# Differential attention of layer 1: when queries, keys and values are loaded, and how many gate steps run beside the first head

## The chip, the core and the metric

One core of a Trainium2 chip runs the whole program, a two-layer encoder trunk for 2048 tokens of width 1024, in float32. The metric is the device time of one execution in microseconds, as a median of several runs. The engines are named as in the profile: PE multiplies matrices, ACT evaluates functions and copies out of PSUM, DVE reduces and combines, POOL does elementwise work in SBUF, and SP issues the DMA transfers, in one queue and in order.

## The reference

Layer 0 is two kinds of chunked attention and is not touched by the change. Layer 1 is differential attention: each of 8 heads has two score maps, and the second is subtracted from the first with a learned weight.

```
def differential_attention(q1, q2, k1, k2, v, lam):
    ...
        s1 = jnp.einsum('bqhd,bkhd->bhqk', qb1, k1).astype(jnp.float32) * scale
        s2 = jnp.einsum('bqhd,bkhd->bhqk', qb2, k2).astype(jnp.float32) * scale
        p1 = jax.nn.softmax(jnp.where(mask, s1, NEG_INF), axis=-1)
        p2 = jax.nn.softmax(jnp.where(mask, s2, NEG_INF), axis=-1)
        a = p1 - lam * p2
        return jnp.einsum('bhqk,bkhd->bqhd', a.astype(v.dtype), v)
...
    o = rms_norm(o, subln_g) * (1.0 - lambda_init)
    y = (o.reshape(b, s, C_W) * jax.nn.silu(gate)) @ w_out
    return x + y
```

The mask lets a query see every key up to the end of its own chunk of 64 tokens.

## The kernel before

A float32 product is made of three products of rounded parts (`mm3`, lines 214 to 216: high by high, high by low, low by high). For scores it is two, because a query tile holds the same 64 rows twice and a key tile holds high and low parts in its two halves (lines 865 and 866).

Layer 1 has two stages. `_project` normalizes the tokens and makes queries, keys and values, which go to scratch in HBM. `_mix1` does all the rest; it begins where the projection's last matmul ends and is 38% of the program.

In `_mix1` the tokens are four blocks `b` of 512, taken from the last to the first, 3, 2, 1, 0. For each block come the 8 heads `h`. A head needs queries of its block (512 tokens) and all keys and values up to the end of the block, in pieces `z` of 512 tokens: four pieces in block 3, three in block 2. For each of four row tiles `j` of 128 queries and each of two maps `m`, `scores` makes a chunk of up to 128x512 per piece in PSUM (4 banks), DVE takes the row maximum (line 869), ACT the exponential (line 872), and POOL and DVE combine the two maps (lines 893 to 899). `values` then transposes the combined rows on PE (line 912), splits them (lines 915, 916) and multiplies them with the values (lines 919 to 921). `gate` multiplies the result with the gate of the head and normalizes it.

Beside the heads runs a side job, `gates()`: the gate part of the input projection, which `_project` leaves out. For each block it makes 8 columns of 128 outputs. A column is 8 steps of three matmuls (`cG`, lines 214 to 216), one PSUM bank, and a copy by ACT to SBUF (line 1033), which goes to HBM. In a block's last column each step is followed by the loads of two 128x512 tiles of the next block's normalized tokens over those just used (`p1hH<-hH`, `p1hL<-hL`, lines 1027 and 1028): 16 loads of 256 KB, called hidden loads below.

Three things set the order. First, `pace` draws from three generators: `heads()`, the queue of `values`, which trails the scores by `LAG1` units (20 in block 3), and the side job. Progress `u` is the mean of the units of scores and of values done; a head has 58 units in block 3 and 42 in block 2. The table `STAGES1` says how many side steps are to be done at each `u`, straight lines between its points:

```
    STAGES1 = ((0, 0), (600, 288), (780, 360), (1000, 440), (1088, 520))
...
        while sided < share((done + trailed) / 2) and next(side, None):
            sided += 1
```

Second, that order is a priority. A scheduler lays the instructions onto the engines by a model of their durations and moves one ahead when what it needs is free in that model; what it wrote is fixed in the program, and each engine runs its list in order. Third, buffers: a tile has a fixed number of places, and a load into a place waits on SP until the readers of the old content are done. Keys have 4 places for each map (`kp`, tags `k0`, `k1`), which in block 3 is exactly one head's keys; values have 4 pairs (`vp`), queries 2 (`ld`), gate weights 3 pairs of half columns. While SP waits for a place, all that stands behind it in the list waits too.

Before the change, `heads()` calls `load` for all pieces of a head (keys of map 0, keys of map 1, then values, piece by piece, lines 982 to 1000), and then `scores`, which begins with the eight loads of its queries (lines 841 to 847).

Of the kernel before, what the change touches and what calls it, by code (L numbers as in the profile page):

```python
# [11 lines left out]
F32R = mybir.dt.float32r  # L12
# [6 lines left out]
P = 128  # L19
# [3 lines left out]
NTB = 4  # L23
BLK = NTB * P
NB = S // BLK
HD = 64
# [5 lines left out]
def f32(ap):  # L32
    return ap.bitcast(F32)
# [52 lines left out]
class Trunk:  # L86
# [727 lines left out]
    def _mix1(self, es):  # L814
        nc, tc, a, s = self.nc, self.tc, self.a, self.s1
        n = "c"
# [7 lines left out]
        kp = pool("kp", 4)  # L824
# [10 lines left out]

        count = [0]

        def scores(h, b, K, res):

            tok = slice(b * BLK, (b + 1) * BLK)  # L840
            qd = ld.tile([P, 2, BLK], F32R, tag="qd", name=n + "qd")
            ql = ld.tile([P, 2, BLK], F32R, tag="ql", name=n + "ql")
            for m in range(2):
                r = slice(m * HD, (m + 1) * HD)
                for part, q in (("qH", qd), ("qL", ql)):
                    nc.sync.dma_start(f32(q[0:HD, m, :]), s[part][h, r, tok])
                    nc.sync.dma_start(f32(q[HD:P, m, :]), s[part][h, r, tok])
            us = res["u"] = []
            for j in range(NTB):
                t = b * NTB + j  # L850
                nk = (t + 1) * P
                cuts = [(c, min(nk, c + 512)) for c in range(0, nk, 512)]
                nb = len(cuts)
                js = slice(j * P, (j + 1) * P)
                nm, la, e = small("nm", 8), small("la", 8), small("e", 8)
                nm, la, e = (x.rearrange("p (m z) -> p m z", m=2) for x in (nm, la, e))
                l, rl = small("l", 2), small("rl", 2)
                rows = []
                for m in range(2):
                    chunks = []  # L860
                    for z, (c, ce) in enumerate(cuts):
                        wd = ce - c
                        ps = pS.tile([P, 512], F32, tag="S", name=n + "S")[:, :wd]
                        kt = K[z][m]
                        mm(ps, qd[:, m, js], kt[:, :wd], start=True, stop=False)  # L865
                        self.anchor = mm(ps, ql[:, m, js], kt[:, :wd], start=False, stop=True).ins  # L866
                        if ce == nk:
                            nc.vector.memset(ps[0:HD, wd - 64:], NEG)
                        nc.vector.tensor_reduce(nm[:, m, z:z + 1], ps, AX.X, ALU.max, negate=True)  # L869
                        chunks.append((sb if m else pp).tile([P, 512], F32, tag=f"P{m}", name=n + f"P{m}", bufs=6 if m else None))  # L870
                        acc = la[:, m, z:z + 1] if nb > 1 else l[:, m:m + 1]
                        nc.scalar.activation(chunks[z][:, :wd], ps, AF.Exp, bias=nm[:, m, z:z + 1], accum_out=acc)  # L872
                        yield wd / 256
                    rows.append(chunks)
                if nb > 1:
                    top, pe = small("top", 2), small("pe", 8).rearrange("p (m z) -> p m z", m=2)[:, :, :nb]
                    nc.vector.tensor_reduce(top, nm[:, :, :nb], AX.X, ALU.min)
                    for m in range(2):
# [23 lines left out]
        def values(h, b, V, res):  # L902
            us = res["u"]
            O = pO.tile([P, BLK], F32, tag="O", name=n + "O")
            nkt = (b + 1) * NTB
            for kt in range(nkt):
                j0 = max(0, kt - b * NTB)
                wd = (NTB - j0) * P
                tp = ptr.tile([P, 512], F32, tag="tr", name=n + "tr")
                kk = (kt % 4) * P  # L910
                for j in range(j0, NTB):
                    nc.tensor.transpose(tp[:, (j - j0) * P:(j - j0 + 1) * P], us[j][kt // 4][:, kk:kk + P], self.ident)  # L912
# [5 lines left out]
                vH, vL = (v[:, kk:kk + P] for v in V[kt // 4])  # L918
                mm(o, vH, H[:, :wd], start=(kt == 0), stop=False, skip_group_check=True)
                mm(o, vH, L[:, :wd], start=False, stop=False, skip_group_check=True)  # L920
                mm(o, vL, H[:, :wd], start=False, stop=(kt == nkt - 1), skip_group_check=True)
                if kt == 2:
                    while normal:
                        normal.pop(0)()
                yield wd / P
            gate(h, b, O)
# [52 lines left out]
                    split(h, b, o)  # L979
                    yield 1  # L980

        def load(h, i, K, V):

            tok = slice(i * BLK, (i + 1) * BLK)
            ks = []
            for m in range(2):
                k = kp.tile([P, BLK], F32R, tag=f"k{m}", name=n + f"k{m}")
                r, o = slice(m * HD, (m + 1) * HD), slice((1 - m) * HD, (2 - m) * HD)
                nc.sync.dma_start(f32(k[r, :]), s["kH"][h, r, tok])
                nc.sync.dma_start(f32(k[o, :]), s["kL"][h, r, tok])  # L990
                ks.append(k)
            K.append(ks)
            vs = []
            for part in ("vH", "vL"):
                v = vp.tile([P, BLK], F32R, tag=part, name=n + part)
                nc.sync.dma_start(
                    f32(v).rearrange("p (t c) -> p t c", t=NTB), s[part][tok, h * P:(h + 1) * P].rearrange("(t p) c -> p t c", p=P)
                )
                vs.append(v)
            V.append(vs)  # L1000

        room = self.last_hidden
        ended = set()
# [90 lines left out]
        queue = []  # L1094
        at = [NB - 1]

        def heads():
            for b in reversed(range(NB)):
                at[0] = b
                for h in range(8):  # L1100
                    K, V = [], []
                    for i in range(b + 1):
                        load(h, i, K, V)
                    res = {}
                    yield from scores(h, b, K, res)
                    queue.append(values(h, b, V, res))
            queue.append(leave())

        def leave():
# [58 lines left out]
```

## Time and profile before

| | |
|---|---|
| median of three runs | 2955.78 us (2952.22 to 2972.79) |
| the profiled execution | 2951.96 us, of which the span is 2950.2 us |
| PE, DVE, ACT, POOL busy, share of the span | 92%, 65%, 54%, 54% |
| mean granted clock of PE | 0.972 |
| last matmul of the projection begins | 1826.68 us |
| first score of head 0, 1, 2, 3, 4 of block 3 | 1840.48, 1875.51, 1926.21, 1979.29, 2041.03 us |
| first score of head 5, 6, 7 of block 3 | 2093.59, 2143.97, 2196.98 us |
| first score of block 2, of block 1 | 2248.42, 2550.78 us |

Times of single events are microseconds from the start of the span. A busy PE is not PE at its peak: the shown length of a 128x512 matmul is 0.39 us, but the next one begins 0.23 us after it.

### The profile page before, as it was taken

The numbers are of one execution on the slowest core, as the hardware profiler recorded it, in microseconds if no ns is written. First come the engines' busy times: TensorE is split into PE (matmuls) and PEld (weight loads), VectorE is DVE, ScalarE is ACT, GpSimd is POOL, SyncE is SP. The second block draws the span as 40 slices with busy tenths as digits, with TensorE's granted clock in tenths as the row PEclk, the third lists the DMA queues.
The fourth block names the chain that finished last, engine by engine and source line by source line (L and its number), as shares of the span: only waits on it lengthen the run. The fifth ranks groups of instructions, "written<-read, shape, count | busy, mean of one in ns | idle before, by whom it ended". The sixth has DMA issues, their size and how long they took to land.

```text
span 2950.2 us, 45159 instructions
## 1 busy us (share of the span) xinstructions
PE 2718.6 (92%) x13672; PEld 2242.1 (76%) x13672; DVE 1917.2 (65%) x4652; ACT 1593.5 (54%) x4135; POOL 1604.6 (54%) x1966
## 2 busy tenths in 40 slices
PE   6999999988888889899999998889999999899888
PEld 5888888876777788777788886667777777677667
DVE  7752385266677676498818861665766888878752
ACT  4443543367556565243334331666766777778752
POOL 3541251245345343267745650776777878789851
PEclk9999999999999999999999998999999999999999
DMA  4773343669988886475895455576768777668863
GB/s 149 230 250 120 113 147 120 197 192 249 262 214 212 216 217 170 146 270 197 259 302 191 127 162 158 164 217 197 225 193 234 200 225 214 176 169 243 221 215 114
DMA packets 427537, 580.79 MB, mean 197 GB/s; under 512 B 48160, under 2 KB 198688, under 8 KB 427296
## 3 DMA queue, kind: packets, MB, share of 16 engines
q1 hardware_dynamic: 427296, 577.92, 66.7%
q8 instruction: 109, 1.79, 0.3%
q14 instruction: 132, 1.08, 0.1%
HBM read 413.14 MB, written 164.63 MB: 196 GB/s over the span
## 4 chain that ended last, share of the span: by engine, by line
PE 63%; DMA 15%; DVE 11%; ACT 4%; POOL 3%; issue 3%; SPq 2%; DVEq 0%; ACTq 0%; POOLq 0%
PE p1mm L216 4%; PE p1mm L214 4%; PE p1mm L215 4%; PE p0mm L215 3%; PE p0mm L216 3%; PE p0mm L214 3%; PE cS L865 3%; PE ctr L912 3%; PE cS L866 3%; DMA mks<-bkL 2%; PE cO L920 2%; PE cG L214 2%; PE cG L216 2%; PE com L214 2%; DVE cnm L869 2%
## 5 line engine op out<-in xcount | busy, mean ns | idle before, releaser
L872 ACT ACTIVATE cP<-cS,cnm 128x512 f32<-128x512 f32 (+3 forms) x640 | 399.0, 630 | 173.8 <-DVE cnm L869 96.0
L869 DVE TENSOR_REDUCE cnm<-cS 128x1 f32<-128x512 f32 (+3 forms) x640 | 374.3, 600 | 100.6 <-PE cS L866 95.4
L865 PE MATMUL cS<-ck,cqd 128*128 128x512 f32 (+3 forms) x640 | 262.9, 415 | 60.0 <-ACT cP L872 20.5
L304 POOL TENSOR_TENSOR p0wL<-p0ws,p0wH 128x512 fp32r<-128x512 f32 (+1 forms) x128 | 155.3, 1246 | 276.0 <-ACT p0wH L303 266.4
L216 PE MATMUL p1mm<-p1wH,p1hL 128*128 128x512 f32 x768 | 303.3, 395 | 0.0
L215 PE MATMUL p1mm<-p1wL,p1hH 128*128 128x512 f32 x768 | 302.9, 395 | 0.4 <-POOL p1wL L304 0.4
L214 PE MATMUL p1mm<-p1wH,p1hH 128*128 128x512 f32 x768 | 302.3, 395 | 0.8 <-ACT p1wH L303 0.8
L899 POOL TENSOR_TENSOR cP<-cP,cP 128x512 f32<-128x512 f32 (+3 forms) x256 | 285.2, 1135 | 0.3
L304 POOL TENSOR_TENSOR p1wL<-p1ws,p1wH 128x512 fp32r<-128x512 f32 x128 | 168.0, 1333 | 136.8 <-ACT p1wH L303 97.5
L214 PE MATMUL p0mm<-p0wH,p0hH 128*128 128x512 f32 (+1 forms) x640 | 237.6, 374 | 3.5 <-ACT p0vt L454 2.6
L866 PE MATMUL cS<-ck,cql 128*128 128x512 f32 (+3 forms) x640 | 235.3, 372 | 3.3 <-DMA cql<-qL 3.3
L215 PE MATMUL p0mm<-p0wL,p0hH 128*128 128x512 f32 (+1 forms) x640 | 238.2, 373 | 0.0
L216 PE MATMUL p0mm<-p0wH,p0hL 128*128 128x512 f32 (+1 forms) x640 | 237.7, 372 | 0.1
L916 DVE TENSOR_TENSOR cptL<-ctr,cptH 128x512 fp32r<-128x512 f32 (+1 forms) x320 | 190.7, 599 | 62.4 <-ACT cptH L915 61.4
L865 PEld LDWEIGHTS cS<-ck,cqd 128*128 128x128 f32 x640 | 123.2, 193 | 104.4 <-ACT cP L872 51.2
L915 ACT ACTIVATE cptH<-ctr 128x512 fp32r<-128x512 f32 (+1 forms) x320 | 169.6, 539 | 58.2 <-PE ctr L912 57.0
L893 POOL TENSOR_SCALAR cP<-cP,ccs 128x512 f32<-128x512 f32 (+3 forms) x288 | 191.9, 683 | 0.0
L912 PE MATMUL ctr<-ident,cP 128*128 128x128 f32 x1088 | 175.4, 277 | 1.4 <-POOL cP L899 1.2
L898 POOL TENSOR_SCALAR cP<-cP,ccs 128x512 f32<-128x512 f32 (+3 forms) x256 | 174.0, 693 | 0.0
L214 PEld LDWEIGHTS p1mm<-p1wH,p1hH 128*128 128x128 f32 x768 | 145.3, 189 | 29.9 <-ACT p1wH L303 1.2
L215 PEld LDWEIGHTS p1mm<-p1wL,p1hH 128*128 128x128 f32 x768 | 145.2, 189 | 29.9 <-POOL p1wL L304 0.8
L216 PEld LDWEIGHTS p1mm<-p1wH,p1hL 128*128 128x128 f32 x768 | 145.4, 189 | 29.3 <-issue 0.2
(321 smaller groups left out, 7719.0 us busy)
## 6 DMA issues: line engine op xcount, KB each, us to landing
p1ws<-in_od_w_in_dram SPq DMA_DIRECT2D x56, 512.0 KB, 4.7
p0ws<-in_ev_w_in_dram SPq DMA_DIRECT2D x48, 512.0 KB, 4.3
ck<-kH SPq DMA_DIRECT2D x160, 128.0 KB, 4.0
ck<-kL SPq DMA_DIRECT2D x160, 128.0 KB, 4.2
cvH<-vH SPq DMA_DIRECT2D x80, 256.0 KB, 3.9
cvL<-vL SPq DMA_DIRECT2D x80, 256.0 KB, 4.7
cqd<-qH SPq DMA_DIRECT2D x128, 128.0 KB, 4.9
cql<-qL SPq DMA_DIRECT2D x128, 128.0 KB, 4.7
```

Of the source, the lines that this page charges most:

```text
L214: mm(ps, aH, bH, start=first, stop=False)
L215: mm(ps, aH, bL, start=False, stop=False)
L216: mm(ps, aL, bH, start=False, stop=last)
L304: nc.gpsimd.tensor_tensor(l[:, :width], ws[:, k, :width], f32(h[:, :width]), ALU.subtract)
L865: mm(ps, qd[:, m, js], kt[:, :wd], start=True, stop=False)
L866: self.anchor = mm(ps, ql[:, m, js], kt[:, :wd], start=False, stop=True).ins
L869: nc.vector.tensor_reduce(nm[:, m, z:z + 1], ps, AX.X, ALU.max, negate=True)
L872: nc.scalar.activation(chunks[z][:, :wd], ps, AF.Exp, bias=nm[:, m, z:z + 1], accum_out=acc)
L893: nc.gpsimd.tensor_scalar(p1, p1, c1, 1.0, ALU.mult, ALU.mult)
L899: nc.gpsimd.tensor_tensor(p1, p1, p2, ALU.add)
L912: nc.tensor.transpose(tp[:, (j - j0) * P:(j - j0 + 1) * P], us[j][kt // 4][:, kk:kk + P], self.ident)
L916: nc.vector.tensor_tensor(L[:, :wd], tp[:, :wd], f32(H[:, :wd]), ALU.subtract)
```

## The change

Three things are edited. The first head's queries are loaded ahead of its keys, and the loads of a head move into the scores of the head before it, through a function `then` that `scores` calls after each chunk: at the first chunk of row tile 2 the next head's queries; in row tile 3, after each chunk, the next head's keys of that map and piece, and at chunks of map 0 also the values of the present head. So the program's order of the keys is now all pieces of map 0, then all of map 1, which is the order of their use. Last, `STAGES1` gets a point: 45 side steps by `u` = 32, where the line before gave 15.

```
-    STAGES1 = ((0, 0), (600, 288), (780, 360), (1000, 440), (1088, 520))
+    STAGES1 = ((0, 0), (32, 45), (600, 288), (780, 360), (1000, 440), (1088, 520))
...
-        def scores(h, b, K, res):
-
+        def load_q(h, b):
             tok = slice(b * BLK, (b + 1) * BLK)
...
+            return qd, ql
+
+        def scores(h, b, q, K, res, then):
...
                         nc.scalar.activation(chunks[z][:, :wd], ps, AF.Exp, bias=nm[:, m, z:z + 1], accum_out=acc)
+                        then(j, m, z)
                         yield wd / 256
...
-        def load(h, i, K, V):
+        def load_k(h, i, m):
...
+        def load_v(h, i):
...
         def heads():
-            for b in reversed(range(NB)):
+
+
+            order = [(h, b) for b in reversed(range(NB)) for h in range(8)]
+            q, K = load_q(*order[0]), {(i, m): load_k(0, i, m) for m in range(2) for i in range(NB)}
+            for (h, b), nxt in zip(order, order[1:] + [None]):
                 at[0] = b
-                for h in range(8):
-                    K, V = [], []
-                    for i in range(b + 1):
-                        load(h, i, K, V)
-                    res = {}
-                    yield from scores(h, b, K, res)
-                    queue.append(values(h, b, V, res))
+                after, res = [None, {}], {"v": []}
+
+                def then(j, m, z):
+                    if (j, m, z) == (2, 0, 0) and nxt:
+                        after[0] = load_q(*nxt)
+                    if j == NTB - 1:
+                        if nxt and z <= nxt[1]:
+                            after[1][z, m] = load_k(nxt[0], z, m)
+                        if m == 0:
+                            res["v"].append(load_v(h, z))
+
+                yield from scores(h, b, q, K, res, then)
+                queue.append(values(h, b, res))
+                q, K = after
             queue.append(leave())
```

The first place is SP's list where the projection ends. `vH` and `vL` are the projection's own stores of values, `cvH` and `cvL` loads of values, `cqd` and `cql` loads of queries, `cwH` and `cwL` of gate weights. Before:

```order
L996 DMA cvH_21096<-vH_74 128x4x128
L996 DMA cvL_21098<-vL_75 128x4x128
L467 DMA vH_74<-p1vH_21038 128x512
L468 DMA vL_75<-p1vL_21039 128x512
L996 DMA cvH_21106<-vH_74 128x4x128
L996 DMA cvL_21108<-vL_75 128x4x128
L996 DMA cvH_21116<-vH_74 128x4x128
L996 DMA cvL_21118<-vL_75 128x4x128
L996 DMA cvH_21126<-vH_74 128x4x128
L996 DMA cvL_21128<-vL_75 128x4x128
L846 DMA cqd_21130<-qH_70 64x512
L847 DMA cqd_21130<-qH_70 64x512
```

Now, at the same place:

```order
L845 DMA cqd_21090<-qH_70 64x512
L846 DMA cqd_21090<-qH_70 64x512
L467 DMA vH_74<-p1vH_21038 128x512
L468 DMA vL_75<-p1vL_21039 128x512
L845 DMA cql_21091<-qL_71 64x512
L846 DMA cql_21091<-qL_71 64x512
```

The eight loads of values ahead of the first query are gone from here; they stand behind the queries of the second head. After the rows shown come the other four query loads and then the first gate weights.

The second place is PE's list in the first head, third row tile, map 0, second and third piece of keys (`ck0`). Before:

```order
L865 MATMUL cS_21336<-ck0_21100,cqd_21130 128x512
L866 MATMUL cS_21336<-ck0_21100,cql_21131 128x512
L214 MATMUL cG_21151<-p1hH_18326,cwH_21252 128x512
L215 MATMUL cG_21151<-p1hL_18327,cwH_21252 128x512
L216 MATMUL cG_21151<-p1hH_18326,cwL_21254 128x512
L865 MATMUL cS_21345<-ck0_21110,cqd_21130 128x512
L866 MATMUL cS_21345<-ck0_21110,cql_21131 128x512
L865 MATMUL cS_21351<-ck0_21120,cqd_21130 128x384
L866 MATMUL cS_21351<-ck0_21120,cql_21131 128x384
L865 MATMUL cS_21361<-ck1_21093,cqd_21130 128x512
L866 MATMUL cS_21361<-ck1_21093,cql_21131 128x512
```

Now:

```order
L870 MATMUL cS_21386<-ck0_21103,cqd_21090 128x512
L871 MATMUL cS_21386<-ck0_21103,cql_21091 128x512
L214 MATMUL cG_21322<-p1hH_18326,cwH_21323 128x512
L215 MATMUL cG_21322<-p1hL_18327,cwH_21323 128x512
L216 MATMUL cG_21322<-p1hH_18326,cwL_21325 128x512
L870 MATMUL cS_21395<-ck0_21106,cqd_21090 128x512
L871 MATMUL cS_21395<-ck0_21106,cql_21091 128x512
L214 MATMUL cG_21322<-p1hH_18326,cwH_21401 128x512
L215 MATMUL cG_21322<-p1hL_18327,cwH_21401 128x512
L216 MATMUL cG_21322<-p1hH_18326,cwL_21403 128x512
```

One step of gates stood between these chunks; now there is one after each chunk, and two behind the second. In the whole first head there are 110 gate matmuls where there were 39.

The third place is SP's list where the first hidden loads fall among the keys of a head. Before, that is the keys of head 3 (`ck0` map 0, `ck1` map 1). The row right ahead of these is the load of the first half of `ck0_22887`, its third piece of map 0:

```order
L1027 DMA p1hH_18326<-hH_78 128x512
L1028 DMA p1hL_18327<-hL_79 128x512 x2
L1027 DMA p1hH_18326<-hH_78 128x512
L989 DMA ck1_22870<-kH_72 64x512
L996 DMA cvH_22202<-vH_74 128x4x128
L996 DMA cvL_22204<-vL_75 128x4x128
L990 DMA ck1_22870<-kL_73 64x512
L1027 DMA p1hH_18326<-hH_78 128x512
L1028 DMA p1hL_18327<-hL_79 128x512
L989 DMA ck1_22880<-kH_72 64x512
L990 DMA ck1_22880<-kL_73 64x512
L990 DMA ck0_22887<-kL_73 64x512
```

Now the first hidden loads fall one head earlier, among the keys of head 2:

```order
L993 DMA ck0_22205<-kH_72 64x512
L994 DMA ck0_22205<-kL_73 64x512
L993 DMA ck0_22218<-kH_72 64x512
L994 DMA ck0_22218<-kL_73 64x512
L993 DMA ck0_22231<-kH_72 64x512
L994 DMA ck0_22231<-kL_73 64x512
L1033 DMA p1hH_18326<-hH_78 128x512
L1002 DMA cvH_22234<-vH_74 128x4x128
L1002 DMA cvL_22236<-vL_75 128x4x128
L1034 DMA p1hL_18327<-hL_79 128x512
L993 DMA ck0_22250<-kH_72 64x512
L994 DMA ck0_22250<-kL_73 64x512
```

Before, pieces of map 1 and hidden loads stand between the halves of a piece of map 0; now the pieces of map 0 stand together and ahead of map 1, and hidden loads and values stand among them. In the program before, one of three rounds of hidden loads stands among the keys of a head like this; now all three do, in whole or in part, among the keys of heads 2 and 5 of block 3 and of head 0 of block 2. From head 4 of block 2 on, PE's list holds the same work head by head, but for small shifts in block 1 and at the last two heads.

More of the change, by code (lines that the diff above doesn't have):

```diff
@@ L847, in scores @@
                     nc.sync.dma_start(f32(q[HD:P, m, :]), s[part][h, r, tok])
+            return qd, ql
+        def scores(h, b, q, K, res, then):
+            qd, ql = q
             us = res["u"] = []
@@ L863, in scores @@
                         ps = pS.tile([P, 512], F32, tag="S", name=n + "S")[:, :wd]
-                        kt = K[z][m]
+                        kt = K[z, m]
                         mm(ps, qd[:, m, js], kt[:, :wd], start=True, stop=False)
@@ L900, in scores, with values @@
                 us.append(rows[0])
-        def values(h, b, V, res):
+        def values(h, b, res):
             us = res["u"]
@@ L917, in values @@
                 o = O[:, j0 * P:]
-                vH, vL = (v[:, kk:kk + P] for v in V[kt // 4])
+                vH, vL = (v[:, kk:kk + P] for v in res["v"][kt // 4])
                 mm(o, vH, H[:, :wd], start=(kt == 0), stop=False, skip_group_check=True)
@@ L980, in fetch @@
                     yield 1
-        def load(h, i, K, V):
+        def load_k(h, i, m):
             tok = slice(i * BLK, (i + 1) * BLK)
[L985 to L992, printed above, removed]
+            k = kp.tile([P, BLK], F32R, tag=f"k{m}", name=n + f"k{m}")
+            r, o = slice(m * HD, (m + 1) * HD), slice((1 - m) * HD, (2 - m) * HD)
+            nc.sync.dma_start(f32(k[r, :]), s["kH"][h, r, tok])
+            nc.sync.dma_start(f32(k[o, :]), s["kL"][h, r, tok])
+            return k
+        def load_v(h, i):
+            tok = slice(i * BLK, (i + 1) * BLK)
             vs = []
@@ L999, in load @@
                 vs.append(v)
-            V.append(vs)
+            return vs
         room = self.last_hidden
```

## The prediction

> **What bounds the kernel now.** I read first the busy time by stretch, cut at the first score of each head of block 3, since the change acts there. Columns: the stretch, its length, then PE, PE weight loads, DVE, ACT and POOL busy with their instructions, granted clock, share of the DMA engines, GB/s.
>
> ```profile
> 1826.90:1840.48 13.58, 0.17 (x1) 0.03 (x1) 0.69 (x1) 0.60 (x1) 0.00 (x0) 0.58 0.97 251
> 1840.48:1875.51 35.03, 30.19 (x107) 20.34 (x107) 22.28 (x53) 22.48 (x68) 18.02 (x27) 0.87 0.53 162
> 1875.51:1926.21 50.70, 47.54 (x233) 37.90 (x233) 33.69 (x73) 33.54 (x92) 39.47 (x55) 1.00 0.60 172
> 1926.21:1979.29 53.08, 49.51 (x248) 39.50 (x247) 35.58 (x80) 36.18 (x97) 35.94 (x47) 1.00 0.76 214
> 1979.29:2041.03 61.74, 52.58 (x251) 41.70 (x248) 35.53 (x77) 36.65 (x99) 44.60 (x62) 0.92 0.71 201
> 2041.03:2093.59 52.56, 50.01 (x248) 39.20 (x246) 34.70 (x79) 35.84 (x99) 38.94 (x52) 1.00 0.63 179
> 2093.59:2143.97 50.38, 49.84 (x251) 39.75 (x250) 35.40 (x77) 35.53 (x98) 36.17 (x49) 1.00 0.87 270
> 2143.97:2196.98 53.01, 49.91 (x243) 40.11 (x241) 35.67 (x78) 35.50 (x98) 43.20 (x57) 0.97 0.65 181
> 2196.98:2248.42 51.44, 48.12 (x241) 38.68 (x240) 34.33 (x77) 35.96 (x98) 36.74 (x49) 1.00 0.64 182
> 2248.42:2550.78 302.36, 288.86 (x1440) 230.23 (x1440) 245.79 (x525) 216.63 (x605) 239.24 (x330) 0.99 0.75 215
> 2550.78:2950.20 399.42, 354.00 (x1688) 278.26 (x1686) 257.91 (x683) 250.97 (x701) 275.79 (x401) 0.95 0.69 194
> ```
>
> PE is the bound from head 1 on: no other engine is busy over 82% in any of these heads, PE is at 85 to 99%. Three exceptions matter: 13.58 us in which PE does nothing, head 0 with 107 matmuls in 35 us where later heads have some 245 in 50 to 53, and head 3, which takes 61.74 us for the work that head 5 does in 50.38.
>
> Then PE's waits from head 1 on to 2258 (in total, times, longest):
>
> ```profile
> PE cS L865 <- DMA ck<-kL: 17.3, 5, 7.9
> ```
>
> and PE's timeline at the start and at two of these five waits (start, length, instruction, idle time before it and its releaser):
>
> ```profile
> 1819.66 0.39 PE L215 MATMUL p1mm<-p1wL,p1hH 128*128 128x512 f32 x1
> ...
> 1826.68 0.39 PE L216 MATMUL p1mm<-p1wH,p1hL 128*128 128x512 f32 x1
> 1840.48 1.73 PE L865 MATMUL cS<-ck,cqd 128*128 128x512 f32 x4 [13.41 <-DMA cqd<-qH]
> ...
> 1843.86 0.77 PE L214 MATMUL cG<-p1hH,cwH 128*128 128x512 f32 x1 [0.16 <-DMA cwH<-wgH]
> ...
> 1991.08 0.79 PE L865 MATMUL cS<-ck,cqd 128*128 128x512 f32 x1 [7.86 <-DMA ck<-kL]
> ...
> 2045.69 0.30 PE L865 MATMUL cS<-ck,cqd 128*128 128x128 f32 x1 [1.65 <-DMA ck<-kL]
> ```
>
> So PE waits 13.41 us for the first queries, and 17.3 us in five waits for keys, each at the third or fourth piece of a new head: 7.86 in head 3, the other four 2.35 in the mean, in heads 2, 4 (1.65), 6 and 7.
>
> **Part 1, the start.** SP's timeline there, and two pieces of the chain of waits, from issue to landing:
>
> ```profile
> 1827.14 0.37 SPq L996 DMA_DIRECT2D cvH<-vH  x1
> ...
> 1828.15 0.45 SPq L467 DMA_DIRECT2D vH<-p1vH  x1
> ...
> 1834.15 0.84 SPq L846 DMA_DIRECT2D cqd<-qH  x1
> ...
> 1839.62 0.53 SPq L1021 DMA_DIRECT2D cwH<-wgH  x1
> ```
>
> ```profile
> 1834.15 5.45 DMA cqd<-qH
> 1839.62 4.11 DMA cwH<-wgH
> ```
>
> The first load of this stage goes out at 1827.14, right after the last projection matmul: its place is free only then, and in the changed list the queries stand at that very place with the same wait, so they cannot go earlier. They go at 1827.14, two at a time around the two stores of 1828.15. Eight query loads took 1839.62 - 1834.15 = 5.47 us, 0.68 each; the six behind the stores run from about 1829.1 to 1833.0. First scores then come at 1827.14 + 5.45 = 1832.6, 7.9 us earlier; but the gate weights, next in SP's list, go at 1833.0 instead of 1839.62 and land 4.11 later, at 1837.1. What is late next is thus the gate weights, with PE doing a few scores ahead of them. I take their shift, **-6.6 us**, between -5 (queries that land slower among more small transfers) and -7.9. The value loads that leave this place have until the first `values`, 20 units of scores later.
>
> **Part 2, denser gates in head 0.** Eight transposes in the chain of waits, and the gate matmuls alone in head 0 and head 1, by stretch as above (without DVE and POOL):
>
> ```profile
> 1950.35 0.87 PE ctr L912 x8
> ```
>
> ```profile
> 1840.48:1875.51 35.03, 12.70 (x39) 8.31 (x39) 0.58 (x1) 0.87 0.53 162
> 1875.51:1926.21 50.70, 20.23 (x75) 13.84 (x75) 1.77 (x3) 1.00 0.60 172
> ```
>
> A 128x512 matmul takes 0.227 us of PE when the next follows (31 of them from 1819.66 to 1826.68). A head of block 3 has 58 units of 256 columns, two matmuls each: 58 full matmuls, 13.2 us. Head 0 adds 39 gate matmuls, 8.9 us: 22 us of work in 35.03. Head 5 has 13.2, 72 gate matmuls 16.3, values 58 x 128 x 3 columns 9.9, transposes 58 x 0.109 = 6.3, in all 46 us in 50.38, a ratio of 1.09. Head 0 now gets 110 gate matmuls: 13.2 + 25.0 and four transposes 0.4 = 38.6; at 1.09 it is 42, and with some 2 us for the lower clock at its start 44: **+9 us**. The 71 matmuls that it takes over are gone from the heads behind it (the counts are even again by block 2's head 3): 71 x 0.227 = 16.1 us less in heads that PE bounds, **-16**. Three more columns end in head 0, and their copies by ACT, 0.58 each, can hold the single PSUM bank: +1. Net **-6**. The cover is PE's spare 13 us there. If head 0 were bound by its chain of maximum, exponential and PSUM places instead, the matmuls would cost it their 16 us and the net is 0; if the later heads shorten at 1.09 and the clock costs nothing, -10.
>
> **Part 3, keys in the order of need.** That keys come as places come free is not new; SP's own waits show it, and its timeline and the chain of waits at the fourth piece of head 4 show what is:
>
> ```profile
> SPq L989 <- PE cS L866: 50.1, 41, 6.0
> ```
>
> ```profile
> 2036.16 1.08 SPq L989 DMA_DIRECT2D ck<-kH  x2
> 2040.94 1.36 SPq L990 DMA_DIRECT2D ck<-kL  x2
> ```
>
> ```profile
> 2041.58 3.97 DMA ck<-kL
> ```
>
> SP stands waiting for key places already. But the first half of the fourth piece (within the pair at 2036.16) went 5.4 us ahead of its second half (2041.58), with three pieces of map 1 between, which are needed later; landing took 3.97, and PE waited 1.65 at 2045.69. The new order puts these halves together. I counted, in both lists, how much PE work stands between the last reading that SP must see before it can issue a key load and that load's first use. Before, the five waits stand where that is 4.1 to 5.2 us (head 5, at 5.0, had none). After, the least by head from head 1 on is 5.8, 4.4, 6.6, 3.9, 5.0, 7.6, 6.6 us and 4.9 for block 2's head 0. So heads 3, 6 and 7 should lose their waits, head 4 keeps one (2.35), and heads 2, 5 and block 2's head 0 are in doubt, because hidden loads now stand among their keys:
>
> ```profile
> 1971.00:1991.00 20.00, 12.22 (x65) 9.92 (x63) 8.71 (x22) 11.37 (x32) 12.07 (x16) 0.88 1.08 260
> ```
>
> ```profile
> 1983.46 1.20 SPq L990 DMA_DIRECT2D ck<-kL  x2
> ```
>
> Where that happened before, the DMA engines were full (share 1.08, 260 GB/s) and the half of head 3's third piece that PE awaited at 1991.08 left SP in the pair at 1983.46. Yet head 5 took its hidden loads at 270 GB/s and was the shortest head, since they came ahead of its successor's keys. With whole pieces in order I take 2.7 for each of the three, near the small waits. After: 2.35 + 8.1 = 10.4 for 17.3, **-7 us**. Bounds: none of the three waits, -15; each waits 7.86, +8.6.
>
> The Trainium skill (DMA: Bandwidth & Descriptors, Specifications) gives about 358 GB/s as a core's limit to HBM; by it the three rounds would not saturate and the term would be nearer -15. The 260 GB/s row at a share of 1.08 speaks against counting on it.
>
> Later queries lose nothing: they wait for the end of the head two before, as they did. From block 2's head 4 on the work by head is the same, and I cost it at nothing.
>
> **Sum.** -6.6 - 6 - 7 = -19.6, so 2951.96 - 19.6 = **2932 us**, on the profiled execution, which is 3.8 under the median of the runs shown and at the level of the fastest (2952.22). From the parts: -5 to -7.9, 0 to -10, +8.6 to -15.
>
> **Rivals.** *All cover holds* (2920): the three rounds cause no wait, -15, head 0 hides its gates at -10, start -6.6, sum -32. For it: head 5 at 270 GB/s without a wait. Against: in head 0 PE's scores wait for ACT to free their four PSUM places, and gates put between them do not make ACT faster.
>
> *Only the start gains* (2945): the loads came at free places already, and the waits for keys merely move to the three heads, with head 0 paying fully for its gates: -6.6. For it: SP's 50.1 us of waiting for places; 17.3 us in three rounds would be 5 each, between the small ones' 2.35 and 7.86. Against: the misplaced halves are a cause by themselves in heads 2, 4, 6 and 7, and that cause goes.
>
> *Hidden loads block the keys* (2973, slower): 16 loads of 256 KB are 4.2 MB, at 260 GB/s 16.1 us. If in each of the three rounds the keys come only behind all of it, the waits are 3 x 16.1 + 2.35 = 50.7 instead of 17.3, +33, less 6.6 and 6: +21. It turns the sign from (17.3 + 12.6 - 2.35) / 3 = 9.2 us a round. For it: 7.86 was reached with one such round. Against: that one also had the split piece.
>
> The Trainium skill (TensorE: Matmul & The Clock Gate, Part 1: The HAM clock gate) says that PE's clock is halved after idle time and comes back after about 3.4 us of work; the rows agree (0.58 in the idle stretch, 0.92 in head 3). By it, keeping each wait under 3.4 us would return another 2 us in head 3, inside the bounds above.
>
> **How the numbers follow.** Forecast 0.46, all cover holds 0.22, only the start gains 0.22, hidden loads block 0.10. The range takes in the first three with their bounds, the forecast's own being 2922 to 2942: 2915 to 2950. A measurement of this kernel can tell about 1%, 29.5 us, from no change. Faster by more needs under 2922.5: about half of "all cover holds" and the forecast's lower end with it, some 0.26. Slower by more, over 2981.5, needs the last rival at its full price and a little more: about half of it and a rest, 0.06. The rest, 0.68, is within 1%.
>
> **What would show it.** Part 1: the first query load at 1827.1, first score near 1832.6, first gate matmul near 1837. Part 2: head 0 of about 44 us with 110 gate matmuls, and PE busy over 90% in it once gates run. Part 3: waits for keys of 8 to 12 us in all, none in heads 3, 6 and 7; heads of block 3 at 1.09 of their matmul work. It is wrong if head 0 takes over 50 us, if any head waits over 6 us for keys, or if the part behind block 2's head 4 (some 543 us) changes by more than 5 us.

## The result, and the profile after

The changed kernel takes 0.9931 of the time before, with a 95% interval from 0.991 to 0.9953: 2943.21 us against 2964.01 us as medians of eight runs each. On the scale of the profiled execution of before (2951.96 us) that is 2931.6 us, 20.4 us less. The profiled execution of the changed kernel took 2939.91 us with a span of 2938.1 us, 12.1 us under the span before. The 2932 us that were forecast, on the scale of 2951.96, meet the ratio to half a microsecond; the terms behind the number do not all hold, as the experiments show.

The busy time by stretch in the changed kernel, cut as before: from the projection's end to the first score; heads 0, 2, 3, 4 and 5 of block 3; block 2; the rest; and the first 13 us of head 0 again. Columns as in the prediction.

```profile
1828.97:1832.74 3.77, 0.00 (x1) 0.04 (x1) 0.69 (x1) 0.60 (x1) 0.00 (x0) 0.92 0.50 168
1832.74:1879.80 47.06, 44.25 (x178) 35.63 (x179) 23.48 (x53) 25.47 (x74) 26.18 (x38) 0.86 0.85 254
...
1929.25:1984.20 54.95, 49.26 (x228) 37.66 (x227) 35.58 (x78) 35.00 (x96) 35.89 (x47) 0.94 0.74 215
1984.20:2034.81 50.61, 48.55 (x243) 38.67 (x242) 36.13 (x76) 35.84 (x97) 42.89 (x59) 1.00 0.59 176
2034.81:2089.19 54.38, 51.82 (x249) 41.35 (x249) 37.88 (x81) 37.41 (x102) 42.35 (x56) 0.97 0.77 216
2089.19:2145.28 56.09, 49.77 (x243) 39.77 (x243) 35.49 (x77) 36.31 (x99) 37.91 (x51) 0.94 0.72 205
...
2242.13:2535.59 293.46, 281.93 (x1411) 227.45 (x1411) 244.24 (x525) 214.20 (x604) 239.08 (x329) 0.98 0.71 205
2535.59:2938.10 402.51, 357.35 (x1688) 282.15 (x1686) 270.02 (x682) 251.28 (x700) 274.22 (x400) 0.94 0.69 192
1832.74:1845.77 13.03, 10.22 (x24) 7.43 (x25) 5.25 (x13) 5.52 (x18) 0.00 (x0) 0.50 0.93 248
```

The idle stretch ahead of the first score went from 13.41 to 3.77 us. Head 0 grew from 35.03 to 47.06 us with 178 matmuls in place of 107; its first 13 us ran at a granted clock of 0.50. Head 3 fell from 61.74 to 50.61 us, and heads 2 and 5 are now long for their work: 54.95 and 56.09 us, with fewer matmuls than head 3 or as many (head 4 takes 54.38 with 249). Block 2 gained 8.9 us, the rest is 3.1 us longer.

SP's timeline at the start shows the queries going out as soon as the projection ends, and the first gate weights behind them:

```profile
1829.04 0.45 SPq L845 DMA_DIRECT2D cqd<-qH  x1
...
1834.39 0.59 SPq L846 DMA_DIRECT2D cql<-qL  x1
1835.03 0.58 SPq L1027 DMA_DIRECT2D cwH<-wgH  x1
```

PE's waits from head 1 on to 2258 (in total, times, longest):

```profile
PE cS L870 <- DMA ck<-kL: 7.0, 5, 3.8
PE cG L214 <- DMA cwH<-wgH: 2.5, 1, 2.5
...
PE cG L216 <- DMA cwH<-wgH: 1.2, 1, 1.2
```

Under this label the waits for keys fell from 17.3 to 7.0 us. Two waits for gate weights are new. The longest wait for keys is in head 5. SP's timeline ahead of it, and PE's:

```profile
2089.45 0.59 SPq L994 DMA_DIRECT2D ck<-kL  x1
2090.13 0.54 SPq L1033 DMA_DIRECT2D p1hH<-hH  x1
2090.76 0.38 SPq L1002 DMA_DIRECT2D cvH<-vH  x1
2091.24 0.46 SPq L1002 DMA_DIRECT2D cvL<-vL  x1
2091.89 0.35 SPq L1034 DMA_DIRECT2D p1hL<-hL  x1
2092.29 0.45 SPq L993 DMA_DIRECT2D ck<-kH  x1
2092.78 0.59 SPq L994 DMA_DIRECT2D ck<-kL  x1
```

```profile
2092.49 0.47 PE L870 MATMUL cS<-ck,cqd 128*128 128x512 f32 x1 [1.40 <-ACT ce L885]
...
2094.03 0.31 PE L925 MATMUL cO<-cptH,cvH 128*128 128x128 f32 x1
2098.17 0.76 PE L870 MATMUL cS<-ck,cqd 128*128 128x512 f32 x1 [3.83 <-DMA ck<-kL]
```

Two hidden loads and two of values, 1 MB, stand between map 0 and the first piece of map 1, which left SP at 2092.78 and was there 5.4 us later. The matmul behind the wait is shown with 0.76 us, where a 128x512 one at full clock has about 0.4: PE had fallen to half its clock.

The wait of 1.40 us at 2092.49 is one for keys as well, though the view names ACT: ACT's `ce` ended only after this matmul had begun, while the key half that SP issued at 2088.25 landed at 2092.35, 0.14 us ahead of it. In the same way the 1.23 us in head 4 (2040.04) and the 2.20 us in block 2's head 0 (2248.48) end 0.09 and 0.14 us after a key half landed. With these three the waits for keys in the changed kernel are 11.8 us; counted so, before has 19.1 us.

### The profile page after: what moved, and what is told of

Same layout as the page of the kernel before. It is cut to its first block, busy times and chain, and to the rows that moved or that the text cites. A ratio compares the mean times of both kernels' runs of the same rounds, so it can differ in the third digit from the quotient of the medians.

```text
span 2938.1 us, 45164 instructions
## 1 busy us (share of the span) xinstructions
PE 2723.6 (93%) x13672; PEld 2252.2 (77%) x13672; DVE 1929.7 (66%) x4652; ACT 1589.6 (54%) x4135; POOL 1606.1 (55%) x1966
## 4 chain that ended last, share of the span: by engine, by line
PE 64%; DMA 13%; DVE 8%; POOL 3%; ACT 3%; issue 2%; SPq 2%; DVEq 0%; ACTq 0%; POOLq 0%
PE p1mm L216 5%; PE p1mm L215 5%; PE p1mm L214 5%; PE cS L870 3%; PE p0mm L216 3%; PE p0mm L214 3%; PE p0mm L215 3%; PE cS L871 3%; PE ctr L918 3%; PE cO L926 2%; PE com L214 2%; PE cG L214 2%; PE com L215 2%; DVE cnm L874 2%; PE cG L216 2%
```

## Experiments

Below, "against before" is the timed ratio with its 95% interval, and the difference in microseconds is that ratio on the median of before in the same comparison. Beside it stand lengths from the one profiled execution of each kernel: the idle stretch ahead of the first score, head 0, and all from head 1's first score to the first score of block 2's head 4, from where PE's list is nearly the same in all kernels. The last column is PE's waits under the label "cS <- DMA ck<-kL" from head 1 to about the start of block 2; waits for keys that a view puts under another label are not in it.

| kernel | against before | us | start | head 0 | heads 1 to (2, 3) | sum | key waits |
|---|---|---|---|---|---|---|---|
| before | 1 | 0 | 13.41 | 35.03 | 531.85 | 580.29 | 17.3 |
| changed | 0.9931 (0.991 to 0.9953) | -20.5 | 3.77 | 47.06 | 511.31 | 562.14 | 7.0 |
| gates alone | 0.9998 (0.9981 to 1.0015) | -0.6 | 13.09 | 45.21 | 523.68 | 581.98 | 22.3 |
| loads alone | 0.9945 (0.9926 to 0.9964) | -16.3 | 3.73 | 39.42 | 525.28 | 568.44 | 6.6 |
| start alone | 1.0012 (0.9996 to 1.0027) | +3.6 | 3.71 | 38.38 | 537.28 | 579.36 | 15.5 |
| key order alone | 0.9969 (0.9952 to 0.9985) | -9.2 | 13.75 | 35.57 | 528.59 | 577.91 | 6.8 |
| before, no hidden loads | 0.9959 (0.9944 to 0.9973) | -12.2 | 13.74 | 35.60 | 525.15 | 574.49 | 8.6 |
| gates, no hidden loads | 0.9916 (0.9893 to 0.9939) | -24.9 | 13.74 | 43.01 | 499.80 | 556.54 | 5.6 |
| loads, no hidden loads | 0.9911 (0.9889 to 0.9934) | -26.4 | 3.75 | 38.08 | 517.69 | 559.52 | 1.2 |
| changed, no hidden loads | 0.985 (0.9818 to 0.9882) | -44.5 | 3.69 | 45.63 | 491.21 | 540.54 | 0.5 |
| changed, small hidden loads | 0.9872 (0.9845 to 0.99) | -37.9 | 3.69 | 46.18 | 496.42 | 546.30 | 3.2 |
| changed, hidden loads by POOL | 0.9993 (0.9976 to 1.001) | -2.1 | 3.66 | 47.71 | 537.45 | 588.82 | 3.8 |
| 52 steps | 0.9898 (0.9876 to 0.992) | -30.2 | 3.78 | 51.34 | 503.25 | 558.37 | 1.0 |
| 55 steps | 0.9893 (0.9865 to 0.9921) | -31.7 | 3.86 | 53.15 | 494.73 | 551.74 | 1.3 |

### The parts, one by one

The gates alone: only the table's line.

```
-    STAGES1 = ((0, 0), (600, 288), ...
+    STAGES1 = ((0, 0), (32, 45), (600, 288), ...
```

> The kernel before with the new point of the gate table alone; queries, keys and values are loaded as before. Theory A (the prediction's sum: each part is worth what it was costed at): the denser gates are worth -6 us by themselves, so about -6 against before. Theory B (head 0 pays for its gates): in the profile of the changed kernel head 0 grew by 12.0 us, not 9, while the gates taken from the heads behind are worth 16; here the first gate matmul stays as late as before (the queries still come last), so head 0 has less idle time to hide them, and by the order all three rounds of hidden loads now fall among keys whose halves are still split; then the net is between 0 and +6. A reading between -2 and 0 would not separate them.

Measured 0.9998, nothing (-5.6 to +4.4 us): the time alone hardly parts the theories. Head 0 grew by 10.2 us, heads 1 to block 2's head 3 fell by only 8.2. PE's waits in this kernel:

```profile
PE cS L865 <- DMA ck<-kL: 22.3, 7, 9.0
```

All three rounds of hidden loads now stand among keys with split halves, and one wait alone is 9.0 us, where the prediction's sum has only gains. The lengths and the waits speak for theory B.

The loads alone: the changed kernel with the old table.

```
-    STAGES1 = ((0, 0), (32, 45), (600, 288), ...
+    STAGES1 = ((0, 0), (600, 288), ...
```

> The changed kernel with the gate table of before: queries first, keys in the order of use, gates as thin in head 0 as before. Theory A (sum): start -6.6 and keys -7, together -13.6, some 6 us slower than the changed kernel. Theory B (rounds of hidden loads among the keys take back what the order of the keys gives): with the old table only the round of head 3 falls among keys, the other two stand ahead of the keys; so the keys give more here, 17.3 us of waits down to about 4, -13, with the start -6.6 to -8 it is -20 to -21, as fast as the changed kernel without any denser gates.

Measured -16.3 us (-11 to -22), which holds both theories. Its key waits, 6.6 us, are nearly all head 3's round.

The start alone: the kernel before, with the first head's queries in front.

```
+                    first = (h, b) == (0, NB - 1)
+                    q = load_q(h, b) if first else None
                     for i in range(b + 1):
-                        load(h, i, K, V)
+                        load(h, i, K, None if first else V)
...
+                        if V is not None and j == NTB - 1 and m == 0:
+                            load_v(h, z, V)
```

> The kernel before with one edit: the first head's queries are loaded ahead of its keys, its values during its last row tile; all other heads load as before, and the gate table is the old one. Theory A: the start alone, -6.6 (-5 to -7.9); first score near 1833, first gate weights issued near 1833 to 1835. Theory C (the start is given back: the clock is still low and the gates come late, so head 0 only stretches): the first score comes 8 us earlier but the first score of head 1 moves by less than 3 us, and the time by 0 to -3.

Measured 1.0012: no gain, as in theory C. But it is not head 0 that gives the time back. From the projection's end, head 1 begins 42.1 us later (3.71 + 38.38) where it was 48.4 before, 6.3 us sooner and about what was costed. Head 1 then takes 56.51 us instead of 50.70. PE's timeline shows the place, DVE's and POOL's the cause:

```profile
1895.82 0.80 PE L868 MATMUL cS<-ck,cqd 128*128 128x512 f32 x1 [4.85 <-ACT cP L875]
```

```profile
1878.29 1.17 DVE L901 SCALAR_TENSOR_TENSOR cP<-cP,ccs,cP 128x512 f32<-128x512 f32 x1 [0.61 <-POOL cP L898]
...
1890.73 4.17 DVE L901 SCALAR_TENSOR_TENSOR cP<-cP,ccs,cP 128x512 f32<-128x512 f32 x1
```

```profile
1890.65 3.71 POOL L904 TENSOR_TENSOR cP<-cP,cP 128x512 f32<-128x512 f32 x3
```

DVE's combination of two rows, 1.17 us in the first row shown, took 4.17 us, from just after POOL began three combinations in a row to just after it ended them; ACT's next exponential waited 3.66 us for that row, PE 4.85 us for ACT. The Trainium skill (SBUF — State Buffer, Who interferes with whom) says that DVE and GpSimd share one pair of ports under an exclusive lock; the two rows agree, and here DVE stayed out for three POOL instructions in succession. From 1894.53 PE was at half clock for 6.83 us. From the first score on, before has no combination on DVE above 2.4 us ahead of 2461 us, so the meeting at this moment belongs to this order; but other orders have their own, as one below shows. How the whole time comes to no gain was not tried; behind block 2's head 4 this profile is 8.7 us longer than that of before.

The order of the keys alone: the kernel before with

```
-            ks = []
-            for m in range(2):
+            for m in range(2):
+                for i in range(b + 1):
...
+            for i in range(b + 1):
                 vs = []
```

> The kernel before with one edit: a head's loads are written as all pieces of map 0, then all of map 1, then the values; queries, the first head and the gate table stay as they were. It separates the order of the keys from the start. The loads in need order with the old gate table measured -16, the start alone +3.5 (-1 to +8). If the keys carry that: -12 to -18, first score of head 0 as late as before (13 us behind the projection). If the start counts once the keys are in order: -7 to -10, that is 7 less than with the start.

Measured -9.2 us (-4.4 to -14.2), the second case: the order of the keys is worth 9.2, and the rest of the edit of the loads the 7.1 us that separate this from the loads alone. That rest is the start, and also the move of every head's loads into the head before, which no kernel tries by itself. So the start that was worth nothing beside the old order of the keys may count beside the new one; but the two intervals overlap, and only their middles differ by 7.

### The rounds of hidden loads

Four kernels leave out the three rounds of hidden loads; the pairs of them differ as the kernels above do. PE's list stays nearly as it was: up to block 2's head 4, between 2513 and 2547 of some 2560 matmuls are in the same order as with the rounds.

```
                         if c == 7 and b:
-                            nc.sync.dma_start(f32(hH), s["hH"][k, :, before])
-                            nc.sync.dma_start(f32(hL), s["hL"][k, :, before])
+                            pass
```

> The kernel before without the hidden loads (the three rounds of loads of the next block's normalized tokens are left out, so the gates of blocks 2, 1 and 0 are computed from block 3's tokens; the work of the engines is the same). It gives the price of the rounds in the kernel before. By the profile of before one round costs: head 3's wait of 7.86 us and some 5 us for the lower clock behind it, so about -10 to -13 against before; if keys there wait for the place and the split halves and not for the rounds, -2 to 0.

> The kernel before with the new point of the gate table and without the hidden loads (left out as in the run before this one). Theory D (the denser gates are worth the costed -6, and in the run of the gates alone this was eaten by hidden loads that had come among the keys, whose waits grew from 17.3 to about 24 us): 5 to 8 us faster than the kernel before without hidden loads. Theory E (head 0 pays for its gates in full): within 2 us of it.

> The changed kernel with the gate table of before and without the hidden loads. Against the kernel before without hidden loads it shows what the queries first and the keys in the order of use are worth where no round disturbs. Theory F (the order of the keys only helps against rounds): -2 to 0, since the start alone measured no gain. Theory A (the small waits of 2.35 us in heads 2, 4, 6 and 7 come from the split halves by themselves and go, the start counts with what is left): -8 to -14.

> The changed kernel without the hidden loads. Theory B (rounds among keys cost what they wait): its key waits in heads 2 and 5 and in block 2's head 0, 10 us together, and some 6 us of lower clock behind them go: 10 to 16 us faster than the changed kernel, -30 to -36 against before, and as fast as or faster than the kernel with the point at 52. If the rounds cost nothing beyond the waits of keys that were late anyway: -20 to -23, as the changed kernel.

The price of the rounds is 12.2 us in before, 24.3 in the kernel with the gates alone, 10.1 with the loads alone, and 24.0 in the changed kernel. The new point of the gate table moves all three rounds among keys, and with it their price rises by 12 to 14 us, with the old order of keys and with the new. By the intervals of the ratios each of the four prices may be off by 4 to 11 us; the lengths say the same, 5.8, 25.4, 8.9 and 21.6 us. Theory B holds in its direction and not in its size: the changed kernel loses 24 us to its rounds, where B had 10 to 16.

Without the rounds the gates show their gain. They are worth 12.7 us in before and 18.1 in the changed kernel (18.0 and 19.0 by the sums in the table), the loads 14.2 and 19.6 (15.0 and 16.0); by the intervals each may be off by 8 to 12 us. The loads' -14 is at the end of theory A's range: five small waits of 8.6 us together, which are there without any round, go, and so does one of 3.53 us in head 6 that the view puts down to ACT though a key half landed 0.14 us before it ended. The gates are worth two to three times what theory D had, so E falls. Head 0 alone, before and with the denser gates, both without hidden loads:

```profile
1841.83:1877.43 35.60, 31.12 (x108) 21.79 (x108) 22.07 (x53) 22.56 (x68) 18.09 (x27) 0.82 0.52 159
```

```profile
1841.01:1884.01 43.00, 42.60 (x179) 34.62 (x180) 23.84 (x54) 25.75 (x74) 24.85 (x37) 0.93 0.70 218
```

Head 0 pays 7.4 us for 71 more matmuls; PE is then busy for 42.60 of 43.00 us, and its clock is higher. The heads behind it shorten by 25.4 us for the same 71 matmuls, which are worth 16.1 at full pace; PE's idle time in them falls by 7.4 us as well.

Where the price of the rounds sits is seen in heads 2 and 5 of the changed kernel without them, and in its waits for keys:

```profile
1927.40:1975.03 47.63, 45.59 (x227) 35.56 (x227) 35.54 (x78) 34.74 (x96) 36.02 (x47) 1.00 0.66 191
...
2077.83:2126.96 49.13, 48.05 (x244) 38.67 (x242) 35.47 (x77) 35.88 (x99) 38.01 (x51) 1.00 0.65 194
```

```profile
PE cS L870 <- DMA ck<-kL: 0.5, 2, 0.3
```

Head 2 falls from 54.95 to 47.63 us and head 5 from 56.09 to 49.13, with the same matmuls but for one and the clock at 1.00: 14.3 of the 21.6 us by the lengths. From the projection's end to block 2's head 4, by all matmul records, PE stood idle for 32.5 us with the rounds and 20.5 without, and ran at half clock for 34.1 and 10.2 us. The 12.0 us of idle time and half of the 23.9 at half clock make 24, against 21.6 by the table's sums: the half clock costs as much as the idle time. All but 3.4 of the 23.9 us lie in heads 2, 4 and 5 and block 2's head 0, each stretch beginning in or right behind a wait for keys or gate weights.

Is it the loads' bytes, or SP held by them? Two kernels bear on this. One cuts each hidden load to 16 columns and keeps its place and its wait:

```
-                            nc.sync.dma_start(f32(hH), s["hH"][k, :, before])
+                            nc.sync.dma_start(f32(hH[:, 0:16]), s["hH"][k, :, few])
```

> The changed kernel with each hidden load cut to 16 of its 512 columns (the rest is left out, so the gates of blocks 2, 1 and 0 are computed mostly from block 3's tokens): the 48 loads keep their places in SP's list and their waits for PE, and 97% of their bytes are gone. Theory G (the rounds' bytes delay the keys on the DMA engines): most of what the rounds cost in the changed kernel, 24 us, comes back: -40 to -45 against before. Theory H (the rounds hold SP: each hidden load waits there for the gate step that reads its place, and the keys behind it go late): the time stays near that of the changed kernel, -20 to -25.

Measured -37.9 us (-30 to -46): of 24 us, 17 come back with the bytes, some 6 or 7 stay. The bytes are most of it (theory G); the remainder may be SP's waits, but the intervals do not settle that. PE's list up to block 2's head 4 is the changed kernel's, matmul for matmul. The other kernel issues the loads from POOL:

```
-                            nc.sync.dma_start(f32(hH), s["hH"][k, :, before])
+                            nc.gpsimd.dma_start(f32(hH), s["hH"][k, :, before])
```

> The changed kernel with the hidden loads issued by POOL in place of SP; the bytes are the same. Theory H (held SP): SP is free for the keys, the waits for keys in heads 2 and 5 and in block 2's head 0 go, up to 24 us faster than the changed kernel, less what POOL's own work loses while POOL waits for the gate steps. Theory G (bytes): the keys are as late as before, within 5 us of the changed kernel, or slower by what POOL loses.

Measured -2.1 us, 18 slower than the changed kernel. Head 2 took 67.43 us. POOL's timeline and PE's waits there:

```profile
1929.73 0.54 POOL L1034 DMA_DIRECT2D p1hL<-hL  x1 [1.02 <-PE cG L216]
1930.70 0.54 POOL L1033 DMA_DIRECT2D p1hH<-hH  x1 [0.43 <-PE cG L216]
1932.15 0.54 POOL L1034 DMA_DIRECT2D p1hL<-hL  x1 [0.92 <-PE cS L871]
```

```profile
PE cG L214 <- DMA cwH<-wgH: 4.0, 2, 3.5
PE cS L870 <- DMA ck<-kL: 3.8, 2, 3.5
...
PE cS L870 <- DMA ck<-kH: 2.1, 1, 2.1
```

Each load now stops POOL's row combinations, and yet in head 2 keys and gate weights are late: a key half that left SP at 1928.73 was under way for 15.21 us, where the one behind the hidden loads above took 5.4. That speaks for the bytes. In head 5 and at the start of block 2, though, no wait for keys above 0.4 us is left, as theory H has it, and POOL's own delay and another order (2364 of 2555 matmuls stand as in the changed kernel) are mixed into the time. So this kernel doesn't part the two theories by itself.

### Rounds ahead of the keys

Last, the changed kernel with only the new point shifted, which moves the rounds and not their size, but also lays PE's matmuls anew (with 52, 1485 of 2555 up to block 2's head 4 stand in the changed kernel's order):

```
-    STAGES1 = ((0, 0), (32, 45), (600, 288), ...
+    STAGES1 = ((0, 0), (32, 52), (600, 288), ...
```

> The changed kernel with 52 side steps in place of 45 at u = 32. By the order this shifts all three rounds of hidden loads to a place ahead of the next head's keys, so that no hidden load stands among keys. Theory B (rounds among keys cost what they wait): the key waits of heads 2, 5 and of block 2's head 0, 2.1 + 5.2 + 2.8 us in the profile of the changed kernel, go; with 21 more gate matmuls in head 0, partly hidden, it is 8 to 12 us faster than the changed kernel, about -28 to -32 against before. Theory A without that: within 2 us of the changed kernel, -20. If head 0 is already full, its 21 more matmuls cost 5 us there and save 5 behind: no change from them.

> The changed kernel with 55 side steps at u = 32: the rounds of hidden loads come still earlier, in the middle of a head, none among keys. If only their distance from the keys counts, it is as fast as with 52 or a little faster, -30 to -34 against before. If head 0 is full (with 52 it took 51.3 us for 40.8 us of matmul work, with waits for gate weights), three more steps there cost their own 2 us and more waits for gate weights, and it is slower than with 52: -22 to -28.

With 52 it is -30.2 us, with 55 -31.7: both beat the changed kernel, by 10 and 11 us, and cannot be told from each other. Their intervals (-24 to -37 and -23 to -40) just overlap that of the changed kernel (-14 to -27), and the one profile with 52 shows 3.8 us of the gain in its lengths, that with 55 10.4; so the gain is likely and its size is not sharp. PE's waits with 52:

```profile
PE cO L926 <- DVE cptL L922: 7.5, 10, 4.0
...
PE cG L214 <- DMA cwH<-wgH: 3.0, 2, 2.2
...
PE cS L870 <- DMA ck<-kL: 1.0, 2, 0.7
```

The waits for keys are nearly gone, and the 10 us are those of theory B. But other waits rise (values waiting for DVE, gate weights). The longest, 3.96 us in head 7, is DVE beside POOL again: a 128x256 combination on DVE took 4.54 us from 2224.69 while POOL made three in a row from 2225.23 to 2228.94, and PE was at half clock for 6.83 us from 2227.97. Besides, 13 to 14 us lie between these kernels and the changed one without hidden loads. So the rounds seem to cost something ahead of the keys as well; how much of it is the other pace of the gates was not parted. With 55 head 0 takes 53.15 us and is not too full: its further steps are gained back behind it.

## Why the prediction was right, point by point

**The start.** The mechanism is the forecast one. The queries went right behind the projection, the first gate weights 6.06 us behind its end (1835.03 - 1828.97) instead of 12.55: a shift of 6.5, forecast 6.6. But the first gate matmul began at 1841.21, not near 1837: 12.2 us behind the projection where it was 16.8, 4.6 us sooner. Alone the start brought nothing, 1.0012; beside the new order of keys it may have a part in the 7.1 us. What this term left out is who comes next: not only gate weights but a clock that stays at 0.50 until 1845.8 (1846.1 before), and in the kernel with the start alone the row combinations of head 1.

**The denser gates.** Forecast +9 in head 0 and -16 behind it. Head 0 took 47.06 us for the 44 forecast; against the loads alone, where it starts as early, that is 7.6 for the gates. Where no hidden load disturbs, head 0 pays 7.4 and 7.6 us, and the heads behind gain 25 and 26 (525.15 to 499.80, 517.69 to 491.21). The term -6 was mis-sized: -12.7 and -18.1 by the timed pairs and 18.0 and 19.0 by the lengths, outside its bounds of 0 and -10. The forecast took the removed matmuls at 0.227 us each, 16.1 in all. With them went idle time of PE in these heads, 7.4 us in one pair and 5.1 in the other, and in the second pair the 10.2 us at half clock, worth 5.1: 16.1 + 5.1 + 5.1 is 26.3 of its 26.5. Why the waits go with the matmuls was not tried.

**The keys.** Waits for keys were forecast at 10.4 us and measured 7.0 under their label, 11.8 with those under other labels, none of them in heads 3, 6 and 7, as said; from 19.1 us that is a fall of 7.3 for the forecast 7. The order alone measured -9.2 for the forecast -7. The bound on head 0 (50 us) and that on a head's waits (6 us) held; head 5 came close with 5.7.

**The rounds.** This step failed: it took 2.7 us, "near the small waits", as the whole price in each of the three heads with hidden loads among their keys. Three times 2.7 for the 7.86 of head 3 before is a net of +0.2 us, hidden in the term -7; the whole price of the rounds rose from 12.2 us to 24.0, a net of +11.8. As lengths the waits were near: 2.1, 5.7 and 2.8 us in the three heads, 10.6 for 8.1. But the prediction priced a wait at its length; it left out the clock behind it and the gate weights that come late in the same crowd. The Trainium skill (TensorE: Matmul & The Clock Gate, Part 1: The HAM clock gate) was read so that a wait under 3.4 us keeps the clock. Here it does not; by stretch, the 3.41 us behind head 2's wait of 2.09 us at 1937.28:

```profile
1937.93:1941.34 3.41, 3.41 (x10) 2.62 (x9) 1.18 (x3) 0.78 (x2) 2.39 (x5) 0.50 1.10 302
```

Not every short wait is paid so: before, the waits of 2.50, 1.65 and 2.39 us in heads 2, 4 and 7 left those heads at 1.00. Ahead of the wait shown, PE had been busy for only 1.19 of the 3.20 us from 1934.00.

**The sum.** The forecast was -13.7 for start and keys with the rounds set apart (-6.6, and 9.4 us of small waits down to 2.35), -6 for the gates, +0.2 for the rounds. Measured, in the order loads, gates, rounds, it is -14.2, -18.1 and +11.8, together -20.5. So the first term holds, and the two others are wrong by 12 us each and cancel: the number came out right partly by luck. The +11.8 may itself be off by some 12 us; that the rounds' price rose with the new point rests on both pairs and on the lengths (+19.6 and +12.7). Of the rivals, "hidden loads block the keys" named the true loss, 12 us where it had 33; "all cover holds" (-32) is close in number to what 55 steps give, where no hidden load stands among keys. The part behind block 2's head 4 is 4.2 us longer in the profile (547.0 for 542.8), within the 5 allowed; kernels with the same list there differ as much (from 538 to 548 us by the last matmul), so it is not put down to the change.

## What to carry to other kernels

A change in the pace of a side job also moves its transfers: look where each burst of loads lands in the issue queue, not only which engine has room for the work. A wait on the bounding engine is often paid twice here, by its length and by the half clock behind it, so removing small waits can be worth more than their sum. And when a forecast comes out right, test its terms: one moved number, 45 to 52, took the change from -20 to about -30 us, and the failed term pointed to it.

## What was not expected of the hardware

One combination on DVE took 4.17 us instead of 1.17 beside three consecutive POOL combinations of 3.71 us together, and in that profile head 1 was 5.8 us longer, against 6.3 us gained ahead of it. With 52 steps the same took 4.54 us in place of the 0.9 us or so of a 128x256 one. A wait of PE of 2.09 us was followed by 3.41 us at half clock. And at the start PE stayed at half clock for 13 us of scores in which it was shown busy for 10.22 of 13.03 us.
